# Opening of a two-layer hybrid trunk: the first chunk loaded ahead of the modulation weights, squares summed by TensorE, products over half of the features begun early

## The chip, the cores and the metric

The kernel runs on one core of a Trainium2 chip. The metric is the time of one execution on the device in microseconds. The kernel before took 3089.61 us, the median of three runs (3087.49 to 3091.21).

## What is computed

Two layers of a trunk over 1024 latent tokens and 256 context tokens of 1024 features. What matters here is the start of a layer: a modulation is computed from a condition vector, the tokens are normalised and modulated, and the result goes through one large input projection. All arithmetic is float32.

```python
def rmsnorm(u, g):
    y = u32 * lax.rsqrt(jnp.mean(u32 * u32, axis=-1, keepdims=True) + EPS)
    return y * g

def modulation(cond, w_mod, b_mod):            # w_mod: 1024 x 3072
    m = jax.nn.silu(cond) @ w_mod + b_mod
    shift, scale, gate = jnp.split(m, 3, axis=-1)

for l in range(DEPTH):                         # 2 layers
    sh_l, sc_l, gt_l = modulation(c, w_mod[l], b_mod[l])
    sh_c, sc_c, gt_c = modulation(c_ctx, w_mod[l], b_mod[l])
    h_lat = rmsnorm(x, norm_g[l]) * (1.0 + sc_l) + sh_l
    h_ctx = rmsnorm(ctx, norm_g[l]) * (1.0 + sc_c) + sh_c
    q_l, k_l, v_l, ga_l, u_l, gb_l, gm_l = split_proj(h_lat @ w_in[l])
    q_c, k_c, v_c, ga_c, u_c, gb_c, gm_c = split_proj(h_ctx @ w_in[l])
    # attention with normalised, rotated q and k; a gated linear recurrence; merge; residual
```

## The kernel before, in words

Features lie on the 128 partitions, in KT = 8 feature tiles; tokens are the columns, in three chunks: C (256 context tokens), L0 and L1 (512 latent tokens each). A float32 product is made of three matmuls of a rounded format: every operand is split into a high and a low part (`whi`, `wlo` for a weight tile, the two tiles of `H[c]` for a chunk), and `gemm` issues high x high, high x low and low x high for each of the 8 feature tiles. In the profile the products of the first projection are `qps`, the split chunks are `h` (latent) and `c` (context).

The order of TensorE's instructions is the order in which the program writes them. It is planned by hand with `Timeline`: `tl.now` is a planned time that every matmul moves on by a cost written in `mm`, `tl.at(delay, fn)` puts a step on a heap with a due time, `pump` and `fill` write the steps that are due between the matmuls of a stream, `drain` writes what is left. The other engines' instructions are ordered by the framework, by when their inputs are ready. All transfers go out on SP's queue.

The opening of layer 0 is in the pool "prep". `load_wm` brings w_mod's first 2048 columns in eight pieces of 512 rows x 512 columns (1 MiB each, four buffers), two pieces for each block of 512 columns; the blocks come in the order 0, 2, 1, 3: shift of features 0 to 511, scale of the same features, shift of 512 to 1023, scale of these. `modulation` multiplies a piece with the condition (`mod_half`, four matmuls in four column groups, `modps`), `mod_turn` copies the finished row (`mrow`, ScalarE) and a step 1 us later turns it onto the partitions with four matmuls (`modpt`); `mod_done` adds the bias and forms the factors.

`load_x` loads a chunk in two halves of four feature tiles. The loads go out in the order w_mod 0, 1, 2, L0, w_mod 3, 4, 5, C, w_mod 6, 7, the first weight tile, L1. `scale_rows` squares the feature tiles (ScalarE), adds the squares up over the tiles (`sq_add`, VectorE, `sqa`), sums them over the partitions with one matmul for 128 tokens (`ssn`), takes the root (`rsqrt_small`, six small instructions), spreads it over the partitions with a matmul for 128 tokens (`rb`) and multiplies the chunk by it (VectorE). `modulate` then applies scale and shift: one ScalarE and two VectorE instructions for a feature tile.

`first_products` is the start of the projection: the first weight tile over L0 and C, the second over L0 and C, then (after the opening) both over L1. Small tiles (`sm`: squares, `mrow`, later `xn`) share three buffers of 128 x 512; PSUM has six banks of the kind "s" (`modps`, `modpt`, `qps`) and two of the kind "av" (`ssn`, `rb`). At the change of layer `norm_chunk` does the same as the opening with other instructions: one VectorE instruction multiplies by factor and root together (L431), ScalarE adds the shift and rounds (L433), VectorE forms the low part (L434).

Of the kernel before, what the change touches and what calls it, by code (L numbers as in the profile page):

```python
# [26 lines left out]
F32 = mybir.dt.float32  # L27
F32R = mybir.dt.float32r
AF = mybir.ActivationFunctionType
# [10 lines left out]
KT = 8  # L40
# [18 lines left out]
def r32(ap):  # L59
    return ap.bitcast(F32)  # L60
# [40 lines left out]
def trunk_kernel(ctx: ExitStack, tc: tile.TileContext, xT, cc, par, wmod, win, wgate, wo,  # L101
# [23 lines left out]
    def gbank(name):  # L125
        banks["i"] += 1
        return ptile(banks["order"][banks["i"] % len(banks["order"])], name)

    def mix(name):
        return ring.tile([128, 1286], F32, name=name, tag="mix", bufs=4)  # L130

    def sm(name, dt=F32):
        return ring.tile([128, 512], dt, name=name, tag="sm", bufs=3)

    def mm(o, a, b, start, stop, cost=None):
        n = 1
# [133 lines left out]
    def w_split(i):  # L270
        if i < len(seq) and i not in ready:
            w_load(i)
            hi = wpool.tile([128, KT, 128], F32R, name="whi", tag="whi")
            lo = wpool.tile([128, KT, 128], F32R, name="wlo", tag="wlo")
            for h, raw in enumerate(raws[i]):
                split(hi[:, 4 * h:4 * h + 4], lo[:, 4 * h:4 * h + 4], raw, weng[0], "v")
            ready[i] = hi, lo

    def w_next():

        i = pos[0]
# [50 lines left out]
    def modulation(l, b, half, wm, box):  # L332
        if half == 0:
            box["ps"] = ptile("s", "modps")
        mod_half(box["ps"], half, wm, 512)
        tl.pump()
        if half == 1:
            mod_turn(l, 4 * b, 4, box["ps"], 1.0)

# [37 lines left out]
    def htile(tag, n):  # L377
        return hpool.tile([128, KT, n], F32R, name=tag, tag=tag, bufs=1)
# [192 lines left out]
    def first_products(g):  # L571

        g.parts = [[c for c in g.chs if c != "L1"], ["L1"]]
        i0, w0 = w_next()
        w_split(i0 + 1)
        tl.at(3.5, lambda: w_load(i0 + 2))
        yield from g.products(0, [c for c in g.chs if c != "L1"], w0)
        i1, w1 = w_next()
        yield from g.products(1, [c for c in g.chs if c != "L1"], w1)
        yield "half"  # L580
        yield from g.products(0, ["L1"], w0)
        w_ahead(i1)
        yield from g.products(1, ["L1"], w1)
# [2 lines left out]
    for l in range(DEPTH):  # L586
        layer_dram(l)
    groups = make_groups(0)
    first = first_products(groups[0])

    def weave(a, b, rate):
        for i, x in enumerate(a):
# [4 lines left out]

    def take_half(gen):
        for x in gen:
            if x == "half":  # L600
                return
            yield

    use_banks("g", "s")
    with tc.tile_pool(name="prep", bufs=1, reuse_waits="tile") as work:
        xs, arrive, scaled = {}, {}, set()
        mod_start(0)
        blocks = (0, 2, 1, 3)

        def load_x(c, k):  # L610
            off, n = CH[c]
            if c not in xs:
                xs[c] = work.tile([128, KT, n], F32, name="xs" + c)
            DMA.dma_start(xs[c][:, k:k + 4], xT[:, k:k + 4, off:off + n])

        def load_wm(i):
            wm = work.tile([128, 4, 512], F32, name="wm", tag="wm", bufs=4)
            r0, c0 = (i % 2) * 512, blocks[i // 2] * 512
            DMA.dma_start(wm, wmod[0, r0:r0 + 512, c0:c0 + 512].rearrange("(k p) n -> p k n", p=128))
            xs[i] = wm  # L620

        def scale_rows(c):

            n = CH[c][1]
            nt = n // 128
            box = {}

            def sums():
                for j in range(KT):
                    sq_add(work, c, j, xs[c][:, j])  # L630
                tl.at(5.0 if c != "C" else 3.5, sums2)

            def sums2():
                ss = ptile("av", "ssn")
                for j in range(nt):
                    mm(ss[:, j:j + 1], sqa[c][:, j * 128:(j + 1) * 128], ones, True, True)
                t = box["t"] = const.tile([128, 4, 4], F32, name="rst", tag="rst", bufs=2)
                rsqrt_small(ss[:, :nt], 1.0 / D, t[:, :, :nt])
                tl.at(2.5, bcast)

            def bcast():
                rb = ptile("av", "rb")
                for j in range(nt):
                    mm(rb[:, j * 128:(j + 1) * 128],
                       box["t"][:, 0, j:j + 1].to_broadcast([128, 128]), ident, True, True)
                for k in range(KT):
                    scaled.add(c)
                    if c == "L1":
                        tl.at(0.5 + 1.4 * k, lambda k=k: late(k, rb))
                    else:  # L650
                        V.tensor_mul(xs[c][:, k], xs[c][:, k], rb[:, :n])

            def late(k, rb):
                V.tensor_mul(xs[c][:, k], xs[c][:, k], rb[:, :n])
                modulate(c, k, 1)

            return sums

        def modulate(c, k0, nk=4):

            assert c in scaled
            n = CH[c][1]
            if k0 == 0:
                H[c] = htile(HS[c][0], n), htile(HS[c][1], n)
            hi, lo = H[c]
            st = 1 if c == "C" else 0
            a, m = mods[0][1], mods[0][0]
            for k in range(k0, k0 + nk):
                S.activation(hi[:, k], xs[c][:, k], AF.Identity, scale=a[:, k, st:st + 1], bias=m[:, k, st:st + 1])
                xn = mix("xn")[:, :n]  # L670
                V.tensor_scalar(xn, xs[c][:, k], a[:, k, st:st + 1], m[:, k, st:st + 1], op0=OP.mult, op1=OP.add)
                V.tensor_sub(lo[:, k], xn, r32(hi[:, k]))  # L672

        clock, tl.now = 2.5, 2.5
        for what in (0, 1, 2, "L0", 3, 4, 5, "C", 6, 7, "w", "L1"):
            if isinstance(what, int):
                clock += 3.3
                load_wm(what)
                arrive[what] = clock
            elif what == "w":  # L680
                w_split(0)
                clock += 1.9
            else:
                for k in (0, 4):
                    load_x(what, k)
                clock += 3.3 if what == "C" else 6.6
                arrive[what] = clock
                tl.n += 1
                heapq.heappush(tl.heap, (clock, tl.n, scale_rows(what)))
        box = {}  # L690
        for i in range(8):
            tl.now = max(tl.now, arrive[i])
            modulation(0, blocks[i // 2], i % 2, xs[i], box)
            if i == 5:
                tl.at(0.0, lambda: modulate("L0", 0))
        tl.at(1.0, lambda: modulate("C", 0))
        tl.at(1.2, lambda: modulate("L0", 4))
        tl.at(4.0, lambda: modulate("C", 4))
        tl.now += 2.0
        tl.fill(take_half(first))  # L700
        tl.drain()

    x_src = {c: (lambda j, c=c: xT[:, j, CH[c][0]:CH[c][0] + CH[c][1]]) for c in CH}
# [663 lines left out]
```

## Time and profile before

| | us |
|---|---|
| median of three runs | 3089.61 |
| lowest and highest | 3087.49, 3091.21 |
| the profiled execution, its own time | 3085.53 |
| its span, first to last instruction | 3083.8 |
| mean granted TensorE clock over the span | 0.990 |

The profiled execution has an instruction record for each engine: PE is TensorE's matmuls, PEld its weight loads, DVE VectorE, ACT ScalarE, POOL GpSimd, SP the queue that issues transfers. A float32 matmul whose operands aren't rounded appears as two instructions. Line 145 (L145) is the helper `mm`, so that matmuls are told apart by the tile they write. "Granted clock" is the share of TensorE's full 2.4 GHz.

### The profile page before, as it was taken

To read this page: it belongs to the slowest core of one execution; us is meant where nothing else is said; L and a number is where in the kernel's file an instruction comes from. 1 tells how busy PE (TensorE), PEld (TensorE's weight loads), DVE (VectorE), ACT (ScalarE), POOL (GpSimd) and SP (SyncE) were. 2 spreads that over 40 slices of the span, in tenths; PEclk is the share of its full clock that TensorE was granted. 3 is DMA by queue.
4 is the path that set the end of the run, shared out by engine and by line. 5 is a ranking of instruction groups with operands and counts; after the bars stand their busy time and mean duration, and the time that the engine had idled before them with its cause. 6 is when DMAs were issued, how large, how long until landed. Compare 5 with 4: busy or idle time off the path is not lost. (4 is left out here: it accounts for less than half of the span.)

```text
span 3083.8 us, 42886 instructions
## 1 busy us (share of the span) xinstructions
PE 2995.5 (97%) x15024; PEld 2380.3 (77%) x15024; DVE 2315.7 (75%) x3610; ACT 1651.4 (54%) x2898; POOL 788.4 (26%) x581
## 2 busy tenths in 40 slices
PE   6999999999999999999999999998999999999999
PEld 4788777777777777888878787776877777777887
DVE  5775777688998998545464785885899999995544
ACT  4325788266666666412233426994666666762222
POOL 0121333244444434200000121322344444440000
PEclk8999999999999999999999999999999999999999
DMA  5444332412212222265565444334212121115554
GB/s 203 141 154 139 92 98 88 137 55 83 66 56 84 62 63 69 91 198 165 188 202 171 140 163 120 98 105 136 71 56 78 56 74 60 53 60 185 184 172 139
DMA packets 255912, 350.98 MB, mean 114 GB/s; under 512 B 74240, under 2 KB 120000, under 8 KB 255440
## 3 DMA queue, kind: packets, MB, share of 16 engines
q1 hardware_dynamic: 255696, 348.25, 36.3%
q8 instruction: 118, 1.93, 0.2%
q14 instruction: 98, 0.80, 0.1%
HBM read 250.44 MB, written 76.58 MB: 106 GB/s over the span
## 5 line engine op out<-in xcount | busy, mean ns | idle before, releaser
L145 PE MATMUL gps<-h,whi 128*128 128x512 f32 x3328 | 1043.7, 395 | 0.2 <-DVE mp L1005 0.2
L145 PEld LDWEIGHTS gps<-h,whi 128*128 128x128 f32 x3328 | 612.1, 189 | 144.5 <-issue 32.0
L1034 DVE TENSOR_TENSOR pl<-pf,ph 128x512 fp32r<-128x512 f32 x656 | 628.6, 959 | 70.8 <-ACT ph L1033 68.0
L145 PE MATMUL gps<-h,wlo 128*128 128x512 f32 x1664 | 654.0, 393 | 10.1 <-DVE wlo L233 10.1
L1032 ACT ACTIVATE pf<-s2ps 128x512 f32<-128x512 f32 x656 | 393.4, 600 | 342.3 <-PE s2ps L145 168.5
L1048 POOL TENSOR_TENSOR acc<-pf 128x512 f32<-128x512 f32 x256 | 353.4, 1380 | 689.0 <-ACT pf L1032 683.4
L1005 DVE TENSOR_REDUCE mp<-s1ps 128x1 f32<-128x512 f32 (+1 forms) x800 | 453.6, 584 | 54.3 <-PE s1ps L145 50.7
L232 ACT ACTIVATE whi<-wraw 128x512 fp32r<-128x512 f32 x392 | 235.4, 630 | 438.8 <-PE gps L145 327.4
L1033 ACT ACTIVATE ph<-s2ps 128x512 fp32r<-128x512 f32 x656 | 389.7, 594 | 0.0
L145 PEld LDWEIGHTS gps<-h,wlo 128*128 128x128 f32 x1664 | 313.6, 188 | 80.7 <-DVE wlo L233 11.4
L233 DVE TENSOR_TENSOR wlo<-wraw,whi 128x512 fp32r<-128x512 f32 x392 | 271.8, 713 | 57.7 <-ACT whi L232 51.2
L145 PE MATMUL s1ps<-k,qa 128*128 128x512 f32 (+1 forms) x800 | 287.0, 368 | 13.5 <-DMA qa<-q0L 7.7
L145 PEld LDWEIGHTS s1ps<-k,qa 128*128 128x128 f32 x800 | 244.5, 309 | 53.2 <-DVE mp L1005 11.6
L145 PE MATMUL avps<-pl,vv 128*128 128x512 f32 x656 | 262.2, 400 | 7.9 <-DVE pl L1034 7.5
L145 PE MATMUL avps<-ph,vv 128*128 128x512 f32 x656 | 266.0, 406 | 0.0
L145 PE MATMUL s2ps<-qa,k 128*128 128x512 f32 x656 | 260.8, 398 | 4.5 <-DVE mp L1005 3.2
L145 PE MATMUL s2ps<-qb,k 65*128 65x512 f32 x656 | 262.3, 400 | 0.2 <-DMA qb<-mr 0.2
L145 PE MATMUL gps<-e,whi 128*128 128x512 f32 x768 | 243.7, 398 | 0.1
L526 POOL TENSOR_TENSOR t<-qg,rc 128x512 f32<-128x512 f32 x40 | 60.8, 1521 | 703.0 <-DMA rc<-in_ropec_dram 511.9
L145 PE MATMUL qps<-h,whi 128*128 128x512 f32 x640 | 203.5, 399 | 3.1 <-DVE h L672 3.0
L1050 POOL TENSOR_TENSOR acc<-acc,pf 128x512 f32<-128x512 f32 x128 | 183.2, 1431 | 80.7 <-ACT pf L1032 78.7
L145 PE MATMUL gps<-c,whi 128*128 128x256 f32 x1024 | 193.6, 286 | 2.7 <-DVE c L228 2.0
(197 smaller groups left out, 4377.8 us busy)
## 6 DMA issues: line engine op xcount, KB each, us to landing
wraw<-in_win_dram SPq DMA_DIRECT2D x200, 256.0 KB
wraw<-in_wo_dram SPq DMA_DIRECT2D x192, 256.0 KB
wm<-in_wmod_dram SPq DMA_DIRECT2D x32, 512.0 KB
us<-uc SPq DMA_DIRECT2D x32, 320.0 KB
a<-ti SPq DMA_DIRECT2D x32, 320.0 KB
wm<-in_wmod_dram SPq DMA_DIRECT2D x8, 1024.0 KB
rb<-rq SPq DMA_DIRECT2D x64, 128.0 KB
k<-k SPq DMA_DIRECT2D x24, 320.0 KB
```

The costliest lines, as they stand in the source:

```text
L145: nc.tensor.matmul(o, a, b, start=start, stop=stop)
L232: S.activation(dst_hi, src, AF.Copy)
L233: (V if lo_eng == "v" else G).tensor_sub(dst_lo, src, r32(dst_hi))
L526: G.tensor_mul(t1, a, rc[:, o:o + n])
L1005: tl.at(0.3, lambda: V.reduce_max(self.mp[:, j, b:b + 1], ps[:, :n], axis=AX.X))
L1032: S.activation(pf, ps, AF.Exp)
L1033: S.activation(ph, ps, AF.Exp)
L1034: tl.at(1.4, lambda: V.tensor_sub(pl, pf, r32(ph)))
L1048: G.tensor_add(self.acc_tile(x), first, pf)
L1050: G.tensor_add(self.accs[x], self.accs[x], pf)
```

## The change

The loads go out in the order L0, w_mod 0 to 3, the first two weight tiles (the second one into two buffers of the pool "mix"), w_mod 4 to 7, C, L1.

`scale_rows` and `modulate` are replaced by `stats`. A square of a feature tile is no longer added to the others by VectorE; 1.2 us later in the plan TensorE sums it over the partitions, one matmul for 128 tokens of each feature tile, and all 8 feature tiles accumulate in the same PSUM columns. The plan enters 0.11 us for each of these matmuls. Root and spreading are as before. Then `make` forms the high and low part as `norm_chunk` does, one ScalarE and two VectorE instructions for a feature tile.

`opening_products` replaces `first_products` in layer 0: both weight tiles over feature tiles 0 to 3 of L0, which need blocks 0 and 2 of the modulation alone (planned from 23.5 us on), then both over feature tiles 4 to 7 (36.8 us), then C (46 us), then L1. Until each of the three times the steps that are due are written first, and while products are written, steps that come due are written between them. `modulation` no longer writes due steps between a piece's matmuls and the row copy.

```diff
@@ modulation
         mod_half(box["ps"], half, wm, 512)
-        tl.pump()
         if half == 1:
             mod_turn(l, 4 * b, 4, box["ps"], 1.0)
@@
-    first = first_products(groups[0])
+    def opening_products(g):
+        g.parts = [[c for c in g.chs if c != "L1"], ["L1"]]
+        (_, w0), (i1, w1) = w_next(), w_next()
+        ps = [gbank("qps") for _ in range(2)]
+        for k0 in (0, 4):
+            for i, (hi, lo) in enumerate((w0, w1)):
+                xh, xl = H["L0"]
+                for k in range(k0, k0 + 4):
+                    mm(ps[i], hi[:, k], xh[:, k], k == 0, False)
+                    mm(ps[i], hi[:, k], xl[:, k], False, False)
+                    mm(ps[i], lo[:, k], xh[:, k], False, k == KT - 1)
+                    yield
+                if k0:
+                    g.evac(i, "L0", ps[i])
+            yield "more"
+        yield from g.products(0, ["C"], w0)
+        yield from g.products(1, ["C"], w1)
+        yield "more"
+        yield from g.products(0, ["L1"], w0)
+        w_ahead(i1)
+        yield from g.products(1, ["L1"], w1)
+
+    first = opening_products(groups[0])
@@
-        def scale_rows(c):
...
-        def modulate(c, k0, nk=4):
...
+        def stats(c, made):
             n = CH[c][1]
             nt = n // 128
+            b = {}
+
+            def square(k):
+                sq = sm("sq")
+                S.activation(sq[:, :n], xs[c][:, k], AF.Square)
+                tl.at(1.2, lambda: add(k, sq))
+
+            def add(k, sq):
+                if k == 0:
+                    b["ss"] = ptile("av", "ssn")
                 for j in range(nt):
+                    mm(b["ss"][:, j:j + 1], sq[:, j * 128:(j + 1) * 128], ones, k + j == 0, k == KT - 1 and j == nt - 1, 0.11)
+                if k == KT - 1:
+                    t = b["t"] = const.tile([128, 4, 4], F32, name="rst", tag="rst", bufs=2)
+                    rsqrt_small(b["ss"][:, :nt], 1.0 / D, t[:, :, :nt])
+                    tl.at(3.0, bcast)
...
+            def make(k):
+                a, m = mods[0][1], mods[0][0]
+                st = 1 if c == "C" else 0
+                hi, lo = H[c]
+                xn = sm("xn")
+                V.scalar_tensor_tensor(xn[:, :n], xs[c][:, k], a[:, k, st:st + 1], b["rb"][:, :n],
+                                       op0=OP.mult, op1=OP.mult)
+                S.activation(hi[:, k], xn[:, :n], AF.Identity, bias=m[:, k, st:st + 1])
+                V.scalar_tensor_tensor(lo[:, k], xn[:, :n], m[:, k, st:st + 1], r32(hi[:, k]),
+                                       op0=OP.add, op1=OP.subtract)
+
+            for k in range(KT):
+                tl.at((0.65 if n == 512 else 0.4) * k, lambda k=k: square(k))
...
+        made = {"L0": lambda k: 21.0 + 0.6 * k if k < 4 else 30.8 + 0.7 * k, "C": lambda k: 0.0, "L1": lambda k: 0.0}
+        clock = 2.5
+        for what in ("L0", 0, 1, 2, 3, "w", 4, 5, 6, 7, "C", "L1"):
             if isinstance(what, int):
                 load_wm(what)
+                clock += 2.7
+                due(clock, lambda i=what: mod(i))
             elif what == "w":
+                w_load(0)
+                raws[1] = [mix("wraw")[:, 0:512].rearrange("p (k n) -> p k n", k=4) for _ in range(2)]
+                for h, raw in enumerate(raws[1]):
+                    DMA.dma_start(raw.rearrange("p k n -> p (k n)"), seq[1][:, 512 * h:512 * h + 512])
+                clock += 2.8
+                due(clock, lambda: (w_split(0), w_split(1)))
             else:
+                load_x(what)
+                clock += 2.7 if what == "C" else 5.4
+                due(clock, lambda c=what: stats(c, made[c]))
+        for at in (23.5, 36.8, 46.0):
+            while tl.heap and tl.heap[0][0] <= at:
+                tl.now = max(tl.now, tl.heap[0][0])
+                tl.step()
+            tl.now = max(tl.now, at)
+            tl.fill(take_half(first))
         tl.drain()
```

## Rows read from the trace of the kernel before

**Rows 1.** The page, its parts 1 and 2: TensorE over the span.
```profile
PE 2995.5 (97%) x15024; PEld 2380.3 (77%) x15024; DVE 2315.7 (75%) x3610; ACT 1651.4 (54%) x2898; POOL 788.4 (26%) x581
...
PE   6999999999999999999999999998999999999999
```
**Rows 2.** Windows: busy us of each engine, granted clock, DMA share, GB/s.
```profile
core 0: us, PE busy (x) PEld busy (x) DVE busy (x) ACT busy (x) POOL busy (x), PEclk, DMA share, GB/s
...
35.00:40.00 5.00, 1.50 (x16) 0.97 (x8) 5.00 (x10) 4.08 (x9) 0.00 (x0) 0.83 1.05 389
40.00:45.00 5.00, 0.00 (x0) 0.00 (x0) 4.76 (x11) 1.72 (x5) 0.00 (x0) 0.50 0.57 184
...
90.00:100.00 10.00, 10.00 (x51) 7.87 (x50) 7.70 (x14) 3.31 (x7) 1.20 (x1) 1.00 0.29 94
```
**Rows 3.** Timeline of the opening, TensorE: start, us, instruction, idle before it, releaser.
```profile
start us, us, engine line op out<-in xcount [idle before <-releaser]
...
7.53 1.94 PE L145 MATMUL modps<-wm,csp 128*32 128x512 f32 x8 [7.53 <-DMA wm<-in_wmod_dram]
...
46.23 0.98 PE L145 MATMUL ssn<-ones,sqa 128*128 128x1 f32 x4 [9.73 <-DVE sqa L391]
...
49.88 1.20 PE L145 MATMUL qps<-h,whi 128*128 128x512 f32 x2
...
51.31 1.70 PE L145 MATMUL modpt<-sel,mrow 128*128 128x2 f32 x8
...
95.92 0.39 PE L145 MATMUL qps<-h,wlo 128*128 128x512 f32 x1
```
**Rows 4.** Timeline, TensorE: w_mod pieces, sums, turns and a broadcast.
```profile
23.71 1.93 PE L145 MATMUL modps<-wm,csp 128*32 128x512 f32 x8 [0.79 <-DMA wm<-in_wmod_dram]
...
25.57 1.87 PE L145 MATMUL ssn<-ones,sqa 128*128 128x1 f32 x8
...
27.30 1.85 PE L145 MATMUL modpt<-sel,mrow 128*128 128x2 f32 x8
...
30.37 2.05 PE L145 MATMUL rb<-ident,rst 128*128 128x128 f32 x8 [1.23 <-DVE rst L400]
...
32.35 3.17 PE L145 MATMUL modps<-wm,csp 128*32 128x512 f32 x16
...
35.45 1.05 PE L145 MATMUL modpt<-sel,mrow 128*128 128x2 f32 x8
...
69.40 1.02 PE L145 MATMUL ssn<-ones,sqa 128*128 128x1 f32 x8 [1.43 <-DVE sqa L391]
```
**Rows 5.** Timeline, TensorE: pairs of products, three matmuls from one to the next.
```profile
54.30 1.05 PE L145 MATMUL qps<-h,whi 128*128 128x512 f32 x2
...
55.58 1.05 PE L145 MATMUL qps<-h,whi 128*128 128x512 f32 x2
...
91.38 0.62 PE L145 MATMUL qps<-h,whi 128*128 128x512 f32 x2
...
92.06 0.62 PE L145 MATMUL qps<-h,whi 128*128 128x512 f32 x2
```
**Rows 6.** By tile and by line: count, duration ns min/median/max, first and last start.
```profile
L145 PE MATMUL ssn<-ones,sqa x40: 164/250/373, 25.6 to 1693.1; 128*128 128x1 f32 x40
...
L390 ACT ACTIVATE sq<-xsL x14: 612/620/633, 16.1 to 67.6; 128x512 f32<-128x512 f32 x14
...
L343 ACT ACTIVATE mrow<-modps x4: 597/597/599, 12.1 to 49.2; 128x512 f32<-128x512 f32 x4
...
L431 DVE SCALAR_TENSOR_TENSOR xn<-mL,ma,rb x16: 739/746/749, 1553.5 to 1705.5; 128x512 f32<-128x512 f32 x16
...
L433 ACT ACTIVATE h<-xn,m x16: 710/726/729, 1554.3 to 1706.3; 128x512 fp32r<-128x512 f32 x16
...
L434 DVE SCALAR_TENSOR_TENSOR h<-xn,m,h x16: 739/747/752, 1555.6 to 1707.5; 128x512 fp32r<-128x512 f32 x16
```
**Rows 7.** Windows of 2 us, columns as in rows 2.
```profile
38.00:40.00 2.00, 0.00 (x0) 0.00 (x0) 2.00 (x5) 1.08 (x3) 0.00 (x0) 0.58 1.05 390
...
62.00:64.00 2.00, 2.00 (x14) 1.77 (x14) 2.00 (x7) 0.92 (x2) 0.00 (x0) 0.95 0.01 4
```
**Rows 8.** Timeline, VectorE: the first small instruction of L0's root.
```profile
27.47 0.16 DVE L395 TENSOR_SCALAR rst<-ssn 128x4 f32<-128x4 f32 x1 [5.27 <-PE ssn L145]
```

More of the change, by code (lines that the diff above doesn't have):

```diff
@@ L599, in take_half @@
         for x in gen:
-            if x == "half":
+            if x in ("half", "more"):
                 return
@@ L605, in trunk_kernel, with load_x @@
     with tc.tile_pool(name="prep", bufs=1, reuse_waits="tile") as work:
-        xs, arrive, scaled = {}, {}, set()
+        xs, box = {}, {}
         mod_start(0)
         blocks = (0, 2, 1, 3)
-        def load_x(c, k):
+        def load_x(c):
             off, n = CH[c]
-            if c not in xs:
-                xs[c] = work.tile([128, KT, n], F32, name="xs" + c)
-            DMA.dma_start(xs[c][:, k:k + 4], xT[:, k:k + 4, off:off + n])
+            xs[c] = work.tile([128, KT, n], F32, name="xs" + c)
+            for k in (0, 4):
+                DMA.dma_start(xs[c][:, k:k + 4], xT[:, k:k + 4, off:off + n])
         def load_wm(i):
@@ L620, in load_wm @@
             xs[i] = wm
-        def scale_rows(c):
+        def stats(c, made):
             n = CH[c][1]
             nt = n // 128
[L626 to L634, printed above, removed]
-                for j in range(nt):
[L636 to L639, printed above, removed]
+            b = {}
[6 more added lines that the diff above has]
+                    b["ss"] = ptile("av", "ssn")
+                for j in range(nt):
+                    mm(b["ss"][:, j:j + 1], sq[:, j * 128:(j + 1) * 128], ones, k + j == 0, k == KT - 1 and j == nt - 1, 0.11)
[3 more added lines that the diff above has]
+                    tl.at(3.0, bcast)
@@ L641, in bcast @@
             def bcast():
-                rb = ptile("av", "rb")
+                rb = b["rb"] = ptile("av", "rb")
                 for j in range(nt):
-                    mm(rb[:, j * 128:(j + 1) * 128],
-                       box["t"][:, 0, j:j + 1].to_broadcast([128, 128]), ident, True, True)
+                    mm(rb[:, j * 128:(j + 1) * 128], b["t"][:, 0, j:j + 1].to_broadcast([128, 128]), ident, True, True)
+                H[c] = htile(HS[c][0], n), htile(HS[c][1], n)
                 for k in range(KT):
[L647 to L657, printed above, removed]
-        def modulate(c, k0, nk=4):
[L661 to L672, printed above, removed]
@@ L674, in trunk_kernel @@
-        clock, tl.now = 2.5, 2.5
-        for what in (0, 1, 2, "L0", 3, 4, 5, "C", 6, 7, "w", "L1"):
+                    due(max(made(k), tl.due + 0.5 + 0.2 * k), lambda k=k: make(k))
+            def make(k):
[8 more added lines that the diff above has]
+                                       op0=OP.add, op1=OP.subtract)
@@ new lines, in stats, with due, mod @@
+            for k in range(KT):
+                tl.at((0.65 if n == 512 else 0.4) * k, lambda k=k: square(k))
+        def due(at, fn):
+            tl.n += 1
+            heapq.heappush(tl.heap, (at, tl.n, fn))
+        def mod(i):
+            modulation(0, blocks[i // 2], i % 2, xs[i], box)
+        made = {"L0": lambda k: 21.0 + 0.6 * k if k < 4 else 30.8 + 0.7 * k, "C": lambda k: 0.0, "L1": lambda k: 0.0}
+        clock = 2.5
+        for what in ("L0", 0, 1, 2, 3, "w", 4, 5, 6, 7, "C", "L1"):
@@ L676, in trunk_kernel @@
             if isinstance(what, int):
-                clock += 3.3
                 load_wm(what)
-                arrive[what] = clock
+                clock += 2.7
+                due(clock, lambda i=what: mod(i))
             elif what == "w":
-                w_split(0)
-                clock += 1.9
-            else:
[L684 to L700, printed above, removed]
+                w_load(0)
+                raws[1] = [mix("wraw")[:, 0:512].rearrange("p (k n) -> p k n", k=4) for _ in range(2)]
```

## The prediction

> **What bounds the kernel now.** The page comes first: TensorE is busy 97% of the span, and of the 40 slices only the first one, 77 us, stands at 6 tenths; all others are at 8 or 9 [rows 1]. So the opening is the one place where TensorE lacks work. The windows come next: from 90 us on TensorE is busy 10.00 of 10 us, while in the opening the DMA still moves 389 GB/s at 35 to 40 us and TensorE does nothing at all between 40 and 45 us [rows 2]; at that rate a w_mod piece of 1 MiB takes 2.7 us. The timeline tells why. The first w_mod piece lands at 7.5 us. The longest stall is 9.73 us ahead of the sums of the context chunk, behind VectorE's additions of squares; the first product of the input projection starts at 49.88 us; the last product of the chunk L1 with the second weight tile ends at 95.92 + 0.39 = 96.3 us [rows 3]. From there TensorE is full, and both kernels have the same work ahead of them. **So I price the change by one number: when that last L1 product ends.** A microsecond there is a microsecond of the kernel.
>
> **The two prices of TensorE.** A transposition of a modulation row or a sum over 512 positions is four matmuls, shown as eight instructions, each with a 128x128 float32 weight load and one or two columns. At 25.57 and 27.30 us eight took 1.87 and 1.85 us, at 35.45 and 69.40 us 1.05 and 1.02 us [rows 4]. The granted clock reads 1.00 in the early windows, but the times say otherwise: its first reading that changes is 0.58 at 38 to 40 us, and it is back near full at 62 to 64 us [rows 7]. I take the durations: the lower level, 1.2 GHz, until somewhere between 30 and 35 us, and again from 38 to 62 us. One instruction lasts up to 0.373 us [rows 6], so a run of them goes at (1.87 - 0.37) / 7 = 0.214 us, 1.71 us for a sum of one 512-column feature tile; at the full clock, with 0.25 us for one, (1.02 - 0.25) / 7 = 0.11 us, 0.88 us. Three products of 512 columns take 55.58 - 54.30 = 1.28 us low and 92.06 - 91.38 = 0.68 us high [rows 5]; three of 256 columns I count as half of that. A w_mod piece takes 1.93 us with its tail [rows 4], about 1.75 us in a run, half of that high.
>
> **What the change removes.** VectorE's additions of squares (14 of 512 columns in L0 and L1) and its scaling of the rows leave, and with them the stall of 9.73 us [rows 3]. That is a wait of TensorE, so up to 10 us could be gained. The first products no longer need all of w_mod, so they move ahead. VectorE's own time is no gain by itself.
>
> **What it adds.** Before, squares were added up first and TensorE summed once for each chunk: 4 + 2 + 4 matmuls. After, each of the 8 feature tiles is summed by TensorE: 32 + 16 + 32 matmuls. At the low price that is 8 x 1.71 = 13.7 us for L0, 6.9 for C, 13.7 for L1, 34 us in all; at the high price 7.0 + 3.5 + 7.0 = 17.5 us. Before it was 1.87 + 0.98 + 1.02 = 3.9 us [rows 3, 4]. The code's own schedule enters 0.11 us for such a matmul, that is 0.44 us for a sum: half of what the best row shows. TensorE's instructions go in the written order, so what is queued behind a sum waits for it, w_mod's pieces, transpositions and products included.
>
> **The order on TensorE**, worked out from the due times: three L0 sums, w_mod 0, four sums, w_mod 1, a sum, turn of block 0, w_mod 2, broadcast of L0's root, w_mod 3, turn of block 2; then 24 products of features 0 to 511 with w_mod 4, 5, 6 and block 1's turn between them, w_mod 7, block 3's turn; then the other 24 L0 products with C's sums and L1's sums between them; C's 48 products with L1's broadcast; L1's 48.
>
> **Stage A, to the scale of the first half.** L0 is now first in the queue, so its first half lands at 7.5 us like the w_mod piece of before [rows 3]; a square is 0.62 us [rows 6], and with the hand-over the first sum starts at 8.5 us. The squares (0.62 us each) are faster than the sums, so TensorE runs without a gap: 13.7 (sums) + 7.0 (four w_mod pieces) + 1.7 (turn) + 2.0 (broadcast, row at 30.37 [rows 4]) = 24.4 us, all at the low clock as the rows from 23.71 to 30.37 us show. Then the copy of the row 0.6 us [rows 6] with 0.5 us of hand-overs, the turn 1.9, two small VectorE instructions 0.4: 8.5 + 24.4 + 3.4 = 36.3 us. The root lies beside turn and w_mod piece and costs nothing (it took from 27.47 to 30.37 us with VectorE held up [rows 4, 8]); were that cover gone, 1 to 2 us. Loads are not what ends here: w_mod piece 4 has to wait for the buffer of piece 0 on SP's queue, and behind it stand 5, 6, 7, C and L1; but piece 0 is used by about 15.5 us, with 3 MB still queued ahead, and 5 to 7 are needed only after 39 us. I price that at nothing; if a piece is late, it costs 2 to 3 us.
>
> **Stage B, to the scale of the second half.** Feature tile 0 takes VectorE 0.75, ScalarE 0.73, VectorE 0.75 us [rows 6] and 0.5 of hand-overs: the first product at 39.0 us, 11 us earlier than before. Then 24 products, four pieces, two turns and one row copy: 10.2 + 7.0 + 3.6 + 1.1 = 21.9 us low, 11.9 high. Some 4 us low and then high, as it went with the two w_mod pieces at 32.35 us and the turn behind them [rows 4], makes 13.8 (4 of 21.9 is 18% of the work, the rest is 82% of 11.9), plus 2 us because VectorE delivers a tile only every 1.5 us: 54.8 us, with the small instructions 55.2. Before, the last turn began at 51.31 us [rows 3], so the early start is already spent.
>
> **Stage C, to the last L1 sum.** Tiles 4 to 7: 2.7 us, 57.9 us. Then 24 L0 products (10.2 low, 5.4 high), C's sums (6.9, 3.5), C's broadcast (1.2, 0.6), L1's sums (13.7, 7.0): 32.0 low, 16.5 high. I take the products high and the sums low, 5.4 + 0.9 + 20.6 = 26.9, since sums did not raise the clock at 25 to 30 us: 84.8 us.
>
> **Stage D, to the mark.** One product triple 0.7, six C triples 2.0, L1's broadcast 1.0, tile 0 2.7, then VectorE's pace of 1.5 us a tile (two instructions of 0.75 [rows 6]), 7 x 1.5 + 0.7 = 11.2, and the second weight tile 8 x 0.68 = 5.4: 23.0 us, so 107.8 us. L1's root and the rest of C's products are hidden in it.
>
> **Sum.** 107.8 - 96.3 = +11.5 us. The profiled execution took 3085.5 us (span 3083.8 and 1.7 around it), 4.1 us below the median of 3089.6; it would become 3097.0, and on the median **3101 us**.
>
> **Rivals.**
> 1. *The sums lift the clock.* If weight loads with one column count as work, TensorE is high from about 12 us. Stage A then ends by w_mod piece 3 (fifth after the first half at 7.5, 2.7 us each: about 21 us) at 26 us, B at 42, C with 16.5 plus some 5 us of waits for squares (three buffers shared with the tiles) at 66, D at 90 to 94 us: -6 to -2 us, 3084 to 3087, not slower. Against it: from 23.71 to 29.15 us TensorE was never idle, and the broadcast at 30.37 us still went at the low price [rows 4]. The Trainium skill (TensorE: Matmul & The Clock Gate, Part 1) says that sustained activity releases the throttle; read plainly that is this rival, and the row does not bear it out for weight loads. Chance 0.18.
> 2. *The opening shrinks as its schedule says*, sums nearly free beside loads and products: L1 ends at 80 us or sooner, -16 us or more, 3074. It needs sums of at most 0.4 us, which no row shows. Chance 0.08.
> 3. *Everything stays low*, since sums and waits break up the products: B takes 21.9 + 2, C 32.0: 121 us, +25, 3114. For it: from 46 to 62 us TensorE stayed low with products in between [rows 5, 7]. Chance 0.12.
>
> **How the numbers follow.** My forecast has 0.62, with 3094 to 3108 of its own (+5 to +18, as C is nearer 22 or 32 us). The range takes in most of rival 1 and stops short of 2 and of the far end of 3: 3085 to 3111. A measurement of this kernel can tell about 0.2%, 6.2 us. Slower by more: 0.54 of the forecast and 0.12 of rival 3, 0.66. Within: 0.08 and 0.15 of rival 1, 0.23. Faster: 0.08 and 0.03, 0.11.
>
> **What would show it.** In the profile of the changed kernel: L0's sums in groups of eight instructions at about 1.7 us and unbroken from 8.5 us; the first product near 39 us; block 3's turn near 55 us; L1's sums as the last thing ahead of C's products, ending near 85 us; L1's last product near 108 us; equal windows afterwards. It is wrong if sums take 0.9 us before 30 us (rival 1), if L1's products are done by 85 us (rival 2), or if the difference arises after the opening, which I have priced at nothing.

## The result, and the profile after

| | before | after |
|---|---|---|
| median, runs made side by side | 3088.55 us (3084.88 to 3091.21) | 3109.86 us (3106.23 to 3112.74) |
| ratio after / before | | 1.0069, 95% interval 1.0057 to 1.0081 |
| profiled execution, its span | 3083.8 us | 3106.8 us |

The kernel became slower by 21.3 us (0.69%); 11.5 us were forecast. The page's first part and its slices, PE row, of after, answer [rows 1]: TensorE is as busy as before in share, and the first slice stands at 7 instead of 6 tenths although the kernel is slower.

```profile
PE 3026.1 (97%) x15164; PEld 2411.8 (78%) x15164; DVE 2294.8 (74%) x3565; ACT 1649.9 (53%) x2898; POOL 784.5 (25%) x581
...
PE   7999999899999999999999999998999999999999
```

Windows of after, the stretches of [rows 2] (columns as there). At 40 to 45 us, where TensorE stood still before, it is busy 4.99 of 5 us; but at 90 to 100 us, where it was full before, it lacks 1.8 us.

```profile
35.00:40.00 5.00, 2.52 (x4) 0.98 (x4) 5.00 (x9) 2.71 (x4) 0.00 (x0) 0.72 1.08 369
40.00:45.00 5.00, 4.99 (x16) 2.11 (x16) 1.28 (x2) 0.04 (x1) 0.00 (x0) 0.59 1.04 386
90.00:100.00 10.00, 8.19 (x65) 7.58 (x64) 5.99 (x10) 5.58 (x11) 0.00 (x0) 0.91 0.01 2
```

The timeline of TensorE in after, the stations of the forecast (columns: start, us, instruction, count, idle before it and what released it), to be read beside [rows 3, 4]:

```profile
8.06 5.28 PE L145 MATMUL ssn<-ones,sq 128*128 128x1 f32 x24 [8.06 <-ACT sq L653]
13.27 1.93 PE L145 MATMUL modps<-wm,csp 128*32 128x512 f32 x8
15.13 6.99 PE L145 MATMUL ssn<-ones,sq 128*128 128x1 f32 x32
...
30.89 1.07 PE L145 MATMUL modps<-wm,csp 128*32 128x512 f32 x8
...
36.26 0.51 PE L145 MATMUL qps<-h,whi 128*128 128x512 f32 x1 [2.48 <-ACT h L681]
...
53.01 1.05 PE L145 MATMUL modpt<-sel,mrow 128*128 128x2 f32 x8 [0.72 <-ACT mrow L342]
57.74 1.01 PE L145 MATMUL ssn<-ones,sq 128*128 128x1 f32 x4 [3.67 <-ACT sq L653]
...
73.66 2.74 PE L145 MATMUL ssn<-ones,sq 128*128 128x1 f32 x24
78.15 1.86 PE L145 MATMUL ssn<-ones,sq 128*128 128x1 f32 x8 [1.75 <-ACT sq L653]
...
87.06 1.87 PE L145 MATMUL ssn<-ones,sq 128*128 128x1 f32 x8 [0.78 <-ACT sq L653]
...
102.67 0.87 PE L145 MATMUL ssq<-sqq,sel 128*32 128x192 f32 x8 [4.48 <-ACT qrow L478]
103.47 1.22 PE L145 MATMUL qps<-h,whi 128*128 128x512 f32 x2
...
108.75 0.70 PE L145 MATMUL qps<-h,whi 128*128 128x512 f32 x2
```

Up to 36 us it goes as worked out: sums in unbroken runs, 0.22 us an instruction, 1.75 us a feature tile. Then come two things that stood in no sum: squares that TensorE waits for in the chunks C and L1, and a wait of 4.48 us for a row of the attention's norm, with four product triples at the low price behind it (103.47 to 108.75).

**The mark, corrected.** The forecast put the end of the last L1 product of the second weight tile at 96.3 us in before, by [rows 3]. That row belongs to the next weight tile already. The right sign is the evacuation of that PSUM bank on ScalarE, in before and in after (ScalarE's timeline):

```profile
94.62 0.67 ACT L463 ACTIVATE qg<-qps,gq 128x512 f32<-128x512 f32 x1
```
```profile
117.53 0.67 ACT L462 ACTIVATE qg<-qps,gq 128x512 f32<-128x512 f32 x1
```

The difference is 22.9 us, that of the two spans 23.0 us. So in these two executions the whole loss arises ahead of this point.

### The profile page after: what moved, and what is told of

It is laid out like the page before. It is cut to its first block, busy times and chain, and to the rows that moved or that the text cites. A ratio compares the mean times of both kernels' runs of the same rounds, so it can differ in the third digit from the quotient of the medians.

```text
span 3106.8 us, 43094 instructions
## 1 busy us (share of the span) xinstructions
PE 3026.1 (97%) x15164; PEld 2411.8 (78%) x15164; DVE 2294.8 (74%) x3565; ACT 1649.9 (53%) x2898; POOL 784.5 (25%) x581
```

## The experiments

Three theories went in. **S**: the loss is the 80 sums on TensorE. **B**: it is the three small buffers, which squares, `xn`, `mrow` and `qrow` share, so that TensorE and ScalarE wait for each other in turn. **L**: it is the load order, or the products split in halves. The table has all kernels; "mark" is the start of that evacuation in the profiled run, and its difference to before's 94.62 us stands beside the difference of the medians.

| kernel | median us | minus before, same session | ratio, 95% interval | mark | minus 94.62 |
|---|---|---|---|---|---|
| after | 3109.86 | +21.3 | 1.0069 (1.0057 to 1.0081) | 117.53 | +22.9 |
| e1 sums on VectorE | 3098.38 | +7.7 | 1.0025 (1.0015 to 1.0035) | 99.96 | +5.3 |
| e2 before, sums on TensorE | 3103.59 | +13.0 | 1.0045 (1.0030 to 1.0061) | 109.35 | +14.7 |
| e3 `xn` in place | 3096.48 | +5.8 | 1.0019 (1.0009 to 1.0028) | 103.95 | +9.3 |
| e4 = e1 and e3 | 3094.94 | +4.3 | 1.0015 (1.0006 to 1.0025) | 99.25 | +4.6 |
| e5 = e3, sums twice | 3132.84 | +44.3 | 1.0140 (1.0125 to 1.0155) | 141.51 | +46.9 |
| e6 = e3, dense sums | 3085.82 | -2.7 | 0.9992 (0.9981 to 1.0003) | 94.53 | -0.1 |
| e7 = e4, squares earlier | 3084.14 | -4.4 | 0.9981 (0.9972 to 0.9991) | 89.08 | -5.5 |
| e8 = e6 and e7 | 3085.88 | -2.6 | 0.9992 (0.9983 to 1.0002) | 91.45 | -3.2 |
| e9 = e7, load order | 3080.14 | -10.0 | 0.9972 (0.9959 to 0.9984) | 83.44 | -11.2 |
| e10 = e7, late products | 3082.43 | -7.7 | 0.9974 (0.9965 to 0.9983) | 85.67 | -9.0 |
| e11 = e9, C's squares earlier | 3082.74 | -7.4 | 0.9976 (0.9966 to 0.9985) | 86.22 | -8.4 |
| e12 = after, late products | 3105.11 | +16.9 | 1.0057 (1.0040 to 1.0074) | 113.75 | +19.1 |

Over 13 kernels and 58 us the mark gives the median's difference to within 3.5 us. That one number prices the opening was right. It is no sharper than that: from the mark to the end of the span, with the same work, the profiled executions took between 2984.7 us (e6) and 2998.0 us (e7), so it is luck that 22.9 and 23.0 us agree so closely. Where two intervals of the table overlap, a difference between these two kernels is not clear of the noise by the medians.

**e1, the sums back on VectorE.** VectorE adds the squares as in before, TensorE sums once for a chunk.

```diff
-                sq = sm("sq")
-                S.activation(sq[:, :n], xs[c][:, k], AF.Square)
-                tl.at(1.2, lambda: add(k, sq))
+                sq_add(work, c, k, xs[c][:, k])
+                if k == KT - 1:
+                    tl.at(2.0, total)
...
                 for j in range(nt):
...
+                    mm(b["ss"][:, j:j + 1], sqa[c][:, j * 128:(j + 1) * 128], ones, True, True, 0.11)
...
```

> The changed kernel with one part undone: the squares are added up by VectorE as before and TensorE sums each chunk once; load order, halved products and everything else stay. Theory S (the loss is the 80 sums on TensorE, at the low price 34 us of its order, against 3.9 before): the opening ends 20 to 30 us earlier than in the changed kernel, 3080 to 3090 us, at or below the kernel before. Theory B (the loss is the three small buffers, which squares, row copies and feature tiles share): squares still use them, so 5 us at most, near 3105. Theory L (the loss is the load order or the products split by halves): no gain, 3107 to 3112.

It fell between the theories: 13.6 us of the loss go, but 7.7 stay.

**e2, the same from the other side.** before with the sums of each feature tile on TensorE (`square` and `add` as in the change), nothing else.

```diff
                 for j in range(KT):
-                    sq_add(work, c, j, xs[c][:, j])
...
+                    tl.at((0.65 if n == 512 else 0.4) * j, lambda j=j: square(j))
...
```

> The kernel before with one part of the change alone: every feature tile's squares are summed by TensorE, w_mod still comes first. Theory S: 30 us more work in TensorE's order, part of it in its idle time of the opening (9.7 us behind VectorE's additions, 11.9 us behind w_mod): slower than before by 8 to 20 us, 3097 to 3109. Theory B: here the feature tiles have buffers of their own, so within 4 us of before. Theory L: within 4 us of before, or faster by the stall of 9.7 us.

As S has it, and against B, which expected at most 4 us: the sums alone cost 13 us in a kernel that has nothing else of the change. Its L0 sums stand in one unbroken run of 64 instructions:

```profile
23.11 13.81 PE L145 MATMUL ssn<-ones,sq 128*128 128x1 f32 x64
```

**e3, the buffers.** The normalised tile is written over the loaded one and takes no small buffer.

```diff
-                xn = sm("xn")
+                xn = xs[c][:, k]
```

> The changed kernel with the feature tile xn written in place into the loaded chunk, so that the three small buffers serve squares and row copies alone; the sums stay on TensorE. Theory S: only the wait of 4.5 us ahead of the second row sum and part of the low clock after it go, 3102 to 3107. Theory B: the waits for squares go too (15.9 us of TensorE's waits in the opening, 8.1 of them the first load), 3090 to 3097.

As B has it: 15.5 us less than after, with every sum still on TensorE. TensorE's waits up to 125 us (waited for, us in all, times, longest), first after, then e3:

```profile
PE ssn L145 <- ACT sq L653: 15.9, 7, 8.1
PE ssq L145 <- ACT qrow L478: 4.5, 1, 4.5
```
```profile
PE ssn L145 <- ACT sq L653: 8.3, 1, 8.3
PE qps L145 <- ACT h L681: 3.2, 3, 2.5
...
PE ssq L145 <- ACT qrow L478: 0.6, 1, 0.6
```

Of the waits for squares only the first one is left (the first load), and the wait for `qrow` is down from 4.5 to 0.6 us. ScalarE's timeline of after shows the coupling that e3 undid: block 3's row copy, the tiles of L0, and then one square at a time, each after a sum of TensorE has given a buffer back.

```profile
52.36 0.60 ACT L342 ACTIVATE mrow<-modps 128x512 f32<-128x512 f32 x1 [5.56 <-PE modps L145]
55.29 2.04 ACT L681 ACTIVATE h<-xn,m 128x512 fp32r<-128x512 f32 x3 [2.33 <-DVE xn L679]
57.27 0.42 ACT L653 ACTIVATE sq<-xsC 128x256 f32<-128x256 f32 x1
58.85 0.42 ACT L653 ACTIVATE sq<-xsC 128x256 f32<-128x256 f32 x1 [1.16 <-PE ssn L145]
60.43 0.72 ACT L653 ACTIVATE sq<-xsC 128x256 f32<-128x256 f32 x2 [1.16 <-PE ssn L145]
```

**e4, both:** the edits of e1 and e3 in one kernel.

> Both edits together: VectorE adds the squares, xn is in place. Theory S: the gain of the vector sums and 2 to 7 us more, 3073 to 3085, faster than the kernel before. Theory B: the two gains don't add, as the vector sums bring nothing by themselves: near the kernel with xn in place. Theory L: near 3105.

So the gains of e1 (13.6 us) and e3 (15.5 us) don't add: together 17.0. Either S is wrong once the buffers are apart, or something else ends just below. That something lies below is also seen from e1 to e4: TensorE's wait for `qrow` falls from 6.3 to 1.5 us, and the mark moves by 0.7 us only. Waits of e4 name candidates: the first w_mod piece, which now comes behind L0, and VectorE's additions.

```profile
PE modps L145 <- DMA wm<-in_wmod_dram: 13.9, 2, 13.2
PE qps L145 <- ACT h L679: 5.3, 4, 2.5
PE ssn L145 <- DVE sqa L390: 5.1, 2, 4.7
```

**e5, the price of the sums measured.** e3 with each sum matmul issued twice.

```diff
-                    mm(b["ss"][:, j:j + 1], sq[:, j * 128:(j + 1) * 128], ones, k + j == 0, k == KT - 1 and j == nt - 1, 0.11)
+                    mm(b["ss"][:, j:j + 1], sq[:, j * 128:(j + 1) * 128], ones, k + j == 0, False, 0.11)
+                    mm(b["ss"][:, j:j + 1], sq[:, j * 128:(j + 1) * 128], ones, False, k == KT - 1 and j == nt - 1, 0.11)
...
```

> The kernel with the normalised tile written in place (e3, 3096.5 us), with every one of the 160 sum instructions of TensorE issued twice; nothing else differs, the root takes half of the total. So it measures what the sums cost once the three small buffers are no longer shared. In e3 the sums keep TensorE busy for 30.3 us. If TensorE's sums still set the end (theory S), all of a second set is paid: 25 to 32 us, 3121 to 3129. If TensorE in e3 waits for squares and tiles anyway (theory B), the second set fills these waits, and 0 to 10 us are paid: 3096 to 3107. In between would say that a part of the sums is covered, and how much.

The busy time of the sums (groups by shape, TensorE, up to the mark: busy us, mean ns of one, idle before), e3 and e5:

```profile
L145 PE MATMUL ssn<-ones,sq 128*128 128x1 f32 x160 | 30.3, 320 | 8.3 <-ACT sq L653 8.3
```
```profile
L145 PE MATMUL ssn<-ones,sq 128*128 128x1 f32 x320 | 65.4, 340 | 7.9 <-ACT sq L653 7.9
```

35.1 us more busy time, a mark 37.6 us later, a median 38.5 us further from before: paid in full, and more than S's 25 to 32 us, since most of the second set ran at the low price (340 ns on the mean, 320 in e3). In e3 TensorE has no slack for sums; S holds there. What more sums cost is not what fewer give back, though: e4 won only 4.7 us by the mark and 1.5 us by the median, the latter within the noise, so the next limit lies just below.

**e6, another form of sum.** Squares rounded to the matmul's rounded format, one 512-column matmul with a matrix of ones for each feature tile, then one row copy and four small matmuls for a chunk.

```diff
-                for j in range(nt):
-                    mm(b["ss"][:, j:j + 1], sq[:, j * 128:(j + 1) * 128], ones, k + j == 0, k == KT - 1 and j == nt - 1, 0.11)
+                mm(b["ss"][:, :n], ones_r, sq[:, :n], k == 0, k == KT - 1)
...
```

> e3 (3096.5 us) with the sums in another form on TensorE: the squares are rounded to the matmul's rounded format, one matmul of 512 columns with a matrix of ones replaces four float32 matmuls of one column, and at the end the total row is copied and turned with four matmuls. A matmul of 512 columns in the rounded format takes 0.43 us low and 0.23 us high (a third of the product triple's 1.28 and 0.68), against 1.71 and 0.88: 8 + 4 + 8 tiles take about 8 us at the low price instead of 30, and the three turns add 4 to 6 us. VectorE gets nothing more to do. Theory S (the sums' time on TensorE is what is left of the loss): 22 minus 5 = 17 us less than e3, 3078 to 3084. Theory B (with separate buffers the sums are covered; what is left are late squares and VectorE's tiles): 3093 to 3100. If short dense matmuls lift the granted clock where one-column matmuls do not, the opening's transpositions read at 1.05 instead of 1.85 us before 30 us, and the kernel ends lower still.

8.5 us less against before than e3, half of what S expected. The dense sums take 7.8 + 2.3 us and the turns 3.7, instead of 30.3. What came in their place is in the waits: TensorE has to wait for w_mod again (2.0 us) and longer for L0's tiles (7.1 instead of 4.7 us); and the first sum waits for the matrix of ones, until 9.5 instead of 8.3 us, which is a cost of the edit itself.

The expectation's question on the clock has an answer too: a w_mod piece at 17.18 us and block 0's turn at 19.02 us went at the high price in e6 (1.85 us for that turn in e3), but the next piece was low again. So a share of the 8.5 us can be the clock's; how much was not separated.

```profile
17.18 1.06 PE L145 MATMUL modps<-wm,csp 128*32 128x512 f32 x8
...
19.02 1.05 PE L145 MATMUL modpt<-sel,mrow 128*128 128x2 f32 x8 [0.35 <-ACT mrow L342]
...
21.20 1.93 PE L145 MATMUL modps<-wm,csp 128*32 128x512 f32 x8
```

**e7, the squares ahead of the row copy.** e4, with the steps of C and L1 written earlier, so that ScalarE squares them ahead of block 3's row copy; the totals keep about their planned times.

```diff
-                    tl.at(2.0, total)
+                    tl.at({"L0": 2.0, "C": 4.6, "L1": 8.5}[c], total)
...
-                tl.at((0.65 if n == 512 else 0.4) * k, lambda k=k: square(k))
+                tl.at(0.65 * k if c == "L0" else 0.0, lambda k=k: square(k))
...
-                due(clock, lambda c=what: stats(c, made[c]))
+                due({"L0": clock, "C": 31.5, "L1": 31.6}[what], lambda c=what: stats(c, made[c]))
```

> e4 (3094.9 us: VectorE adds the squares, tiles in place), with the squares of C and L1 put ahead of block 3's row copy in ScalarE's order; the totals stand where they stood on TensorE. In e4 the squares of C begin only at 48.5 us and L1's total is late (TensorE waits 4.7 us for it at 71.6 us). If the order on ScalarE is what is left of the loss (theory B, its second half), those waits and what stands behind them go: 5 to 12 us, 3083 to 3090. If TensorE's own load and low clock is what is left (theory S), or VectorE, which now adds squares in the middle of the tiles of L0, becomes the last: within 3 us of e4, 3092 to 3098, or slower.

8.7 us less against before than e4, as B's second half has it, and the first kernel whose whole interval lies below before. By ScalarE's timelines C's squares begin at 43.23 us (48.47 in e4) and L1's at 46.92 (52.84), all ahead of block 3's row copy at 52.06; in e4 that copy, at 47.97, stood ahead of them. First e4, then e7:

```profile
47.97 0.60 ACT L342 ACTIVATE mrow<-modps 128x512 f32<-128x512 f32 x1 [5.62 <-PE modps L145]
48.47 0.41 ACT L386 ACTIVATE sqa<-xsC 128x256 f32<-128x256 f32 x1
```
```profile
43.23 0.41 ACT L386 ACTIVATE sqa<-xsC 128x256 f32<-128x256 f32 x1
...
52.06 0.60 ACT L342 ACTIVATE mrow<-modps 128x512 f32<-128x512 f32 x1 [0.23 <-DVE sqa L390]
```

TensorE's waits for VectorE's additions, 5.1 us in e4, are gone, for a new wait of 3.9 us ahead of block 3's turn. Loads and the number of sums are the same, so the limit below the sums was the place of C's and L1's squares in ScalarE's order.

**e8, e6 and e7 together**, with the squares written into the chunk's still empty high tile.

```diff
-                sq = sm("sq", F32R)
+                sq = H[c][0][:, k]
...
```

> e6 and e7 together, and no small buffer shared at all: the squares are written into the chunk's high tile, which nobody has written yet, rounded, and summed by dense matmuls on TensorE; C's and L1's squares stand ahead of block 3's row copy. If squares behind the row copy and sums on TensorE are both of what is left of the loss, this takes both away: about 3070 to 3085, faster than the kernel before. If the pace of VectorE's tiles (two instructions of 0.75 us for each) or the granted clock sets the end of the opening by now, it stays at 3090 to 3097 like e3 and e4.

No better than either, and at 3085.9 us between the expectation's two ranges. TensorE's waits now name C's copied row (2.6 us) and L1's root (2.9 us), small steps of the other engines that stand between a total and its broadcast. That the two cures act on the same stretch is how I read it; no run separates it.

**e9, the load order.** e7 with two w_mod pieces loaded ahead of L0; the steps of L0 get the planned time 10.0 us.

```diff
-        for what in ("L0", 0, 1, 2, 3, "w", 4, 5, 6, 7, "C", "L1"):
+        for what in (0, 1, "L0", 2, 3, "w", 4, 5, 6, 7, "C", "L1"):
...
-                due({"L0": clock, "C": 31.5, "L1": 31.6}[what], lambda c=what: stats(c, made[c]))
+                due({"L0": 10.0, "C": 31.5, "L1": 31.6}[what], lambda c=what: stats(c, made[c]))
```

> e7 (3084.1 us) with one thing changed: the loads go out as two w_mod pieces, then L0, then the other pieces, so that TensorE gets a piece at about 7.5 us, as in the kernel before, and not at 13.1 us. Theory L (the load order of the change costs TensorE's first work, and the work that then stands in a row until block 2's turn at 28.4 us is TensorE's): the two pieces and a turn, 1.9 + 1.9 + 1.9 us, leave that row, the squares of L0 come 5 us later but are wanted only at 20 us: the first product 2 to 4 us earlier than 31.97 us, and the kernel 2 to 4 us less, 3080 to 3082. Rival: the loads are the limit anyway, since piece 3 lands at the same time in either order, or the squares of L0 become the last: within 1.5 us of e7, or slower.

5.6 us less against before than e7 by the medians, and as much by the marks, though the two intervals overlap (0.9959 to 0.9984 and 0.9972 to 0.9991), so the size is not sure. TensorE starts at 7.75 us and the first product at 29.68 instead of 31.97 us. Only 2.3 of the 5.6 us are explained by that row; block 3's turn then came 4.5 us earlier (48.24 instead of 52.71 us, by TensorE's timelines) at half the duration, 1.05 instead of 1.87 us, so the clock has a share. That share is read, not tested. First e7's turn, then rows of e9:

```profile
52.71 1.87 PE L145 MATMUL modpt<-sel,mrow 128*128 128x2 f32 x8 [3.88 <-ACT mrow L342]
```
```profile
7.75 1.93 PE L145 MATMUL modps<-wm,csp 128*32 128x512 f32 x8 [7.75 <-DMA wm<-in_wmod_dram]
...
12.93 1.05 PE L145 MATMUL modpt<-sel,mrow 128*128 128x2 f32 x8 [0.73 <-ACT mrow L342]
...
29.68 0.80 PE L145 MATMUL qps<-h,whi 128*128 128x512 f32 x1 [2.95 <-ACT h L679]
...
48.24 1.05 PE L145 MATMUL modpt<-sel,mrow 128*128 128x2 f32 x8 [3.89 <-ACT mrow L342]
```

e9 has the lowest median of this study (e10 and e11 lie within the noise of it): 0.28% under before (0.16 to 0.41%), some 1% under after.

**e10, the early products undone.** e7 with L0's first 24 products put behind the whole modulation.

```diff
-        for at in (23.5, 36.8, 46.0):
+        for at in (36.8, 36.8, 46.0):
```

> e7 (3084.1 us) without the third part of the change: the products over the first half of L0's features are no longer written between the pieces of w_mod, but only behind all of the modulation, like the kernel before did. So it prices the early products alone. In e7 24 products stand between 32 and 47 us, in time in which TensorE has else only four pieces and a turn; put behind block 3's turn they cost 24 x 0.23 = 5.5 us at the high price and 10 us at the low one, and the modulation comes a few us earlier for it, since nothing stands between its pieces. If the early products are worth what the change takes them for: 4 to 9 us more than e7, 3088 to 3093. If the modulation's gain or the loads take it back: within 2 us of e7.

Not 4 to 9 us more but 3.3 us less against before; the intervals of e7 and e10 overlap, so no gain is shown by the medians, only that nothing was lost. TensorE stands idle for 11 us ahead of the turns of blocks 1 and 3, as the rows show, and the profiled run's mark is still 3.4 us earlier: the turn of block 3 begins at 47.20 instead of 52.71 us, all eight tiles of L0 are there, and behind it TensorE waits for only 1.7 us in all.

```profile
36.05 1.87 PE L145 MATMUL modpt<-sel,mrow 128*128 128x2 f32 x8 [4.95 <-ACT mrow L342]
...
47.20 1.87 PE L145 MATMUL modpt<-sel,mrow 128*128 128x2 f32 x8 [6.11 <-ACT mrow L342]
...
49.78 1.20 PE L145 MATMUL qps<-h,whi 128*128 128x512 f32 x2
```

**e11, C's squares earlier still**, on e9: `"C": 26.5` in the line of e7, with C's total kept at its planned time (9.6 instead of 4.6 us behind the squares).

> e9, and C's squares put ahead of the row copy of block 1 too in ScalarE's order, where ScalarE stands idle in e7 (7 us, until 42.7 us). In e7 block 3's row copy waits 3.9 us on TensorE's side for the squares ahead of it on ScalarE; C's eight squares of 0.36 us are 2.9 us of that. If both hold: e9's gain and 2 to 3 us more, 3077 to 3080, 0.3% under the kernel before. If VectorE's additions, which take 9 us in a row in e7, end last instead: as e9.

The wait for block 3's row fell from 3.9 to 2.1 us, and the kernel gained nothing: its median is no lower than e9's. In the profiled runs the difference begins at 13 us, where the first turn took 1.87 us in e11 and 1.05 us in e9, ahead of anything that the edit touches. The row of e11, beside that of e9 at 12.93 us above:

```profile
13.19 1.87 PE L145 MATMUL modpt<-sel,mrow 128*128 128x2 f32 x8 [0.71 <-ACT mrow L342]
```

**e12, the early products undone in the changed kernel itself**, by the edit of e10.

> The changed kernel (3109.9 us) with its third part alone undone: the products over the first half of L0's features stand behind all of the modulation. On top of e7, where VectorE adds the squares, this edit gave 1.7 us (3084.1 to 3082.4 us) and the end of the second weight tile's L1 products came 3.4 us earlier. If early products are worth nothing in this opening, because they hold up block 3's row and with it every later square and tile: 3103 to 3110. If they are worth their TensorE time in the changed kernel, where sums fill TensorE and the idle time is elsewhere: 24 triples at 0.43 us or 0.23 us a matmul come on top, 5 to 10 us, 3115 to 3120.

4.4 us less against before than after, and a mark 3.8 us earlier, as the first of the two expectations has it. The intervals overlap here too. So the third part of the change brought nothing in either setting, and cost some 3 to 4 us in both as far as single profiles tell.

## Why the prediction was right in sign and short in size

The stations, forecast and measured, in us:

| stage | forecast | after |
|---|---|---|
| A: first product | 39.0 | 36.26 |
| B: end of block 3's turn | 54.8 | 54.06 |
| C: last L1 sum ends | 84.8 | 88.93 |
| D: last L1 product ends (0.3 ahead of the evacuation) | 107.8 | 117.2 |
| the same in before | 96.3 | 94.3 |

**A and B held, in part by luck.** Sums of 1.75 us without a gap, as priced at 1.71; the first product came 2.7 us earlier, mostly since the clock rose by 30.89 us (a w_mod piece at 1.07 us, the turn at 32.73 us in 1.05), where I had priced all of stage A low. B took 17.8 instead of 15.8 us, since triples went at the low price until about 44 us, for some 8 us where I had put some 4. The two misses cancel to 0.7 us. "The early start is already spent" by block 3's turn held, and e10 and e12 say more: with it undone no time is lost.

**C failed by 4.9 us.** The step that failed is "the squares (0.62 us each) are faster than the sums, so TensorE runs without a gap". I had stated it for L0, where it is true, and then added up C's and L1's sums as if it held for them too. For C and L1 the squares stand on ScalarE behind block 3's row copy and share three buffers with the tiles. TensorE waited six times, 7.8 us (15.9 less the first 8.1). The first, 3.67 us, lies beside L0's tiles, which I had counted; the other five, 4.1 us, are the term that was missing. Without them the sums and products from 57.74 us on took 88.93 - 57.74 - 4.14 = 27.05 us, forecast 26.9, though from another mixture than I took: half of L1's sums high (73.66: 0.11 us an instruction), most L0 products low; that the two mixtures cost the same is luck. The sum also has one L0 triple twice, 0.7 us: C has all eight of the second half, and D begins with "one product triple". I had the mechanism in rival 1 ("some 5 us of waits for squares") and left it out of the forecast.

**D failed by 5.3 us.** It held no term for a wait for a buffer. The 4.48 us for `qrow`, which sits in one of the same buffers, and the low clock behind that wait (four triples at 1.28 instead of 0.68 us, 2.4 us) make 6.9; the rest of D went 1.6 us faster than forecast, since VectorE had made six of L1's eight tiles by the end of that wait (it began the last two at 102.11 us), where I had let TensorE follow their pace of 1.5 us. In e3, where the tiles hold no small buffer, the wait is 0.6 us.

**The mark of before** was read 2.0 us too late. Together: -2.7 + 2.0 + 4.9 + 5.3 + 2.0 = 11.5 us, which is the 23.0 measured less the 11.5 forecast. The range, 3085 to 3111 us, held by 1.1 us; the measured 3109.86 lies above the 3094 to 3108 that I gave the forecast by itself. With the buffers apart (e3) the last L1 product ends at 103.6 us, against 107.8 forecast and 117.2 in after: my sum, without a wait for a buffer, is nearer to the kernel without the shared buffers, though it is 4 us too high for that one.

**The rivals.** Rival 1 fell: the sums of the opening did not lift the clock (8.06 to 22.1 us at 0.22 us an instruction). The Trainium skill (TensorE: Matmul & The Clock Gate, Part 1) has sustained activity release the throttle; the rows at 8.06 and 15.13 us and the run of 13.81 us in e2 do not bear that out for these sums. Rival 2 fell: no sum took 0.4 us. Rival 3 (+25 us) was near in size but not in kind: products did run high from 44 to 51 us and again from 91 us on but for the four triples behind the wait for `qrow`, B took 17.8 us and not 23.9, and its 25 us had no term for buffers.

**What the loss was, as far as the runs settle it.** Two things that overlap: sums on TensorE (13.6 us by undoing them, 13.0 us when put into before, paid in full in e5) and the shared small buffers (15.5 us by undoing them). Both together give 17.0, because below them lies the place of C's and L1's squares on ScalarE (8.7 us by e7), and below that, as far as overlapping intervals allow, the load order (5.6 us by e9). "Loads are not what ends" was right of after and wrong of the kernels without its sums: in after the first 5.28 us of sums run in the time in which TensorE would otherwise wait for w_mod, which in e4 lands at 13.2 us. That is read from the rows: the load order was undone only on top of e7, never alone in after. How much of e9's and e11's difference is the phase of the clock stays open.

## What to carry to other kernels

When small tiles from several steps share a few buffers, write the wait for a buffer as a term of its own, and follow on each in-order engine which step stands ahead of the one that gives the buffer back. When one undone part gives back most of a loss and another one does too, do both in one kernel: their sum shows the next limit. Work moved to TensorE has to be priced by the durations of its instructions in the trace, not by its count of columns; and an early start of products was worth nothing here (e10, e12), as the step that they delayed was what the rest waited for.

## What the runs showed of the hardware that was not expected

The clock fell within a stretch in which TensorE was never idle. In e3 (timeline, TensorE) 32 one-column instructions went at 0.11 us each, and 24 more, behind one product triple, at 0.21; in e5 112 in a row took 22.43 us, 0.20 each. The granted clock of e3 says the same: 1.00 from 72 to 74 us, 0.81 from 74 to 76, 0.50 from 76 to 78, with TensorE busy 2.00 of 2 us in each window.

```profile
70.81 3.63 PE L145 MATMUL ssn<-ones,sq 128*128 128x1 f32 x32
74.30 0.70 PE L145 MATMUL qps<-h,whi 128*128 128x512 f32 x2
74.84 0.40 PE L145 MATMUL qps<-h,wlo 128*128 128x512 f32 x1
75.08 4.96 PE L145 MATMUL ssn<-ones,sq 128*128 128x1 f32 x24
```
```profile
89.19 22.43 PE L145 MATMUL ssn<-ones,sq 128*128 128x1 f32 x112
```

So in e3 such sums cost twice: their own time, and the price of the products behind them (C's triples took 0.64 us each until 85 us and 0.36 from 86.6 us on, when the clock was back). What else would have brought the clock down there was not tested. And the granted-clock column of a window does not agree with the durations at the start of a run: over 0 to 35 us of after it reads 1.00 (window below), while w_mod pieces at 13.27 and 30.89 us took 1.93 and 1.07 us.

```profile
0.00:35.00 35.00, 24.94 (x120) 18.79 (x120) 3.93 (x23) 11.07 (x18) 0.51 (x5) 1.00 0.89 316
```
